# Transposing queries and keys as unsplit float32 values, two heads to a block, and splitting them from PSUM

## The chip, the cores and the metric

The kernel runs on one core of one Trainium2 chip. The metric is device time in microseconds (us). A core has five engines that work from their own instruction streams, in order, and wait for each other by semaphores: PE (matrix products and transposes, results in PSUM), DVE (vector operations), ACT (activation functions and copies), POOL and SP (here mostly DMA and some adds). PSUM is a small memory of eight banks of 128 x 512 float32 from which DVE and ACT read PE's results.

## The reference

The program is an encoder of two layers on x[512, 1024]. Each layer computes, in float32 accuracy:

```python
xn = rms_norm(x, norm1_g[l])
aq, ak, av, bq, bk, bv, cq, ck, cv, cg, gates = jnp.split(xn @ w_in[l], split_pts, axis=-1)
aq = apply_rope(rms_norm(aq, a_q_norm_g[l]), ...)      # ak, bq, bk in the same way; 64 columns a head
ya = dilated_mixer(aq, ak, av)                         # A: 6 heads, 3 waves of 2
yb = diff_attention(bq, bk, bv, lam)                   # B: 4 heads with two softmax maps each, 4 waves
cq, ck = apply_rope(cq), apply_rope(ck) * 64 ** -0.5   # C: retention, 4 heads, 2 waves of 2
yc = silu(cg) * rms_norm(bidirectional_retention(cq, ck, cv, ...))
g = sigmoid(gates)
x = x + (g0 * (ya @ w_br_a[l]) + g1 * (yb @ w_br_b[l]) + g2 * (yc @ w_br_c[l])) @ w_o[l]
x = x + square(relu(rms_norm(x, norm2_g[l]) @ w_mlp1[l])) @ w_mlp2[l]
```

Scores are products of queries and keys over the 64 columns of a head, so queries and keys must come to PE with those columns on the partitions. They are computed with tokens on the partitions and have to be transposed.

## The kernel before

**Split numbers.** PE takes reduced float32 (fp32r) at full rate. Every large product is therefore done on two parts of each factor, a high part (the value rounded to fp32r) and a low part (the rest): high x high, high x low and low x high, added up in PSUM. Weights arrive by DMA as `raw`; ACT writes `whi` and DVE `wlo` (`refine`, L261), one unit ahead of their use.

**The main stream.** `gemm` (L273) does a chunk of a product: four PSUM banks (`acc`, a pool of four, L125), four units of weights, and a yield after each bank of each unit. In the last unit a bank is evacuated as soon as it is complete. Since a chunk takes all four banks of the pool, the first matmul of the next chunk waits until the first bank of this one has been read. The order of chunks is `sequence` (L810): waves A0, A1, A2, then `cg`, C0, C1, B0, B1, gates and branch products (G, W), B2, B3, G20 and so on. A wave holds queries, keys and values of two heads (of a head with two maps for B).

**The side threads.** The work on a wave runs in four generators per layer: `thread_prep` (L790: statistics, rope and transposes of queries and keys), `thread_a`, `thread_b` (L603) and `thread_c` (L780). They are woven into the main stream when the program is written, not while it runs. `build` (L1024) keeps for each engine a sum of estimated costs (`self.cost`: a DVE operation 0.09 + columns/800, one of ACT 0.19 + columns/1000, an fp32r transpose 0.06, an fp32 one 0.11, in us) and gives out side steps, the threads in turn, as long as DVE and ACT stand more than 3 us behind PE in those sums (`SLACK`). A step that yields `("wait", name)` may go on only when PE's sum has grown by `W[name]` (4.0 for "prep", 8.0 for "yb", 6.0 for "sc").

**The exception to it.** Before wave i the main stream yields `("need", ("done", l, wave i-4))` (`LAG`, L33 and L864). While that is not met, `build` writes side steps with no regard to the sums, first those that may go on, and, where none may, by `step_side(True)`, which also disregards the waits. For B3 the need is that both heads of C1 are done; for B2 it is C0.

**Heads.** A head of C (`c_head`, L753) takes four rounds of scores, decay and products, and then `head_norm` (L568): ACT copies the result out of PSUM (`y`), PE transposes it (`ps_yt`), ACT squares and sums four blocks, DVE makes a reciprocal root in a chain of operations on 128 x 4, then `yn<-ps_yt`; after the wait "yb" PE transposes back (`ps_yb`) and DVE multiplies by the gate. `b_tail` of a head of B ends in the same way.

**The step that is changed.** `prep` (L466) is called 36 times (2 layers, 9 waves, two halves of 256 tokens). DVE applies norm and rope into `o`, [128 tokens, 2 token tiles x 2 (queries, keys) x 2 heads x 64]. ACT and DVE split it into `sp`, laid out so that a head's high and low parts stand side by side in blocks of 128 columns; eight fp32r transposes (L511) fill two PSUM banks, one for queries and one for keys. They are copied into `qk`, which has six planes of [128, 512]: for head m plane m (queries), 2+m (keys) and 4+m (keys with high and low parts exchanged). `score` (L520) multiplies whole planes m and 4+m for the two cross terms and a half of planes m and 2+m for high x high.

Of the kernel before, what the change touches and what calls it, by code (L numbers as in the profile page):

```python
# [9 lines left out]
FT = mybir.dt.float32  # L10
FR = mybir.dt.float32r
AF = mybir.ActivationFunctionType
OP = mybir.AluOpType
# [3 lines left out]
P = 128  # L17
# [46 lines left out]


def weight_plan(sequence):
    """The weight blocks in the order of use: (array, layer, first row tile, row tiles, columns per row tile)."""
    units, chunks = [], {}
    r = lambda a, n: list(range(a, a + n))
    for l in range(DEPTH):  # L70
        for s in sequence:
            kind, k0, k1, name = s[0], 0, KD, "w_in"
            if kind == "A":
                cols = [(x * 384 + s[1] * 128, 128) for x in range(3)]
            elif kind == "B":
                cols = [(1152 + x * 512 + s[1] * 128, 128) for x in range(3)]
            elif kind == "C":
                cols = [(2688 + s[1] * 128, 128), (2944 + s[1] * 128, 128), (3200 + s[1] * 256, 256)]
            elif kind == "cg":
                cols = [(3712, 512)]  # L80
            elif kind == "G":
                cols = [(4224 + s[1] * 1024 + s[2] * 512, 512)]
            elif kind == "W":
                name, cols, k1 = "w_br_" + "abc"[s[1]], [(s[2] * 512, 512)], (3, 4, 4)[s[1]]
            elif kind == "O":
                name, cols = "w_o", [(s[1] * 512, 512)]
            elif kind == "M1":
                name, cols = "w_mlp1", [(s[1] * 512, 512)]
            else:
                name, cols, k0, k1 = "w_mlp2", [(s[2] * 512, 512)], s[1] * 8, s[1] * 8 + 8  # L90
            first = len(units)
            for k in range(k0, k1, 2):
                units.append((name, l, (k, cols), min(2, k1 - k), sum(c for _, c in cols)))
            chunks[l, s] = (first, len(units))
    return units, chunks


def pack_weights(inputs, sequence):
    """Every weight block laid out as it lands on chip: row in the tile, row tile, column."""
    out = []  # L100
    for (name, l, (k, cols), n, c) in weight_plan(sequence)[0]:
        w = inputs[name][l, k * P:(k + n) * P]
# [5 lines left out]
class Trunk:  # L108
    def __init__(self, ctx, tc, a):
# [8 lines left out]
        self.up = mk("u", N_U)  # L118
        self.wp = mk("w", 1)
        self.qp = mk("qk", 2)  # L120
        self.sp = mk("sp", 2)
        self.tp = mk("tiny", 4)
        self.Tp = mk("dec", 1)
        self.dp = mk("scratch", 1, space=bass.MemoryType.DRAM)
# [114 lines left out]
            self.stt(lo, x, scale, hi.bitcast(FT), OP.mult, OP.subtract)  # L239
        return hi, lo  # L240

    # ---------------------------------------------------------------- weights
    def plan(self):
        units, self.ch = weight_plan(self.sequence)
        self.units, off = [], 0
# [52 lines left out]
                yield  # L298
            k += n

    # ---------------------------------------------------------------- set-up
    def setup(self):
        nc, a = self.nc, self.a
        cp = self.cp
# [73 lines left out]
                self.stt(S[:, :, 0:8], bc(g[:, 8:16]), -1.0, self.sinp, OP.mult, OP.mult)  # L378
                self.tt(S[:, :, 8:16], bc(g[:, 0:8]), self.sinp, OP.mult)

    # ---------------------------------------------------------------- norm of x
    def norm_open(self, which, l):
        self.nrm = {"col": which * 16 + l * 8, "xg": [None] * KD, "sq": None}

# [35 lines left out]
        self.act(rB, b2)  # L420
        return rB

    # ---------------------------------------------------------------- prep of q, k, v
    def wave_buffers(self, kind):
        w = {"kind": kind}
        w["qk"] = self.qp.tile([P, 6, SEQ], FR, tag="qk", name=self.uid("qk"))
# [39 lines left out]
    def prep(self, w, jp):  # L466
# [5 lines left out]
        if w["kind"] in "AB":  # L472
# [11 lines left out]
            o = u  # L484
            self.tt(u8, u8, rs[:, :, None].to_broadcast([P, 8, 64]), OP.mult)
        else:
# [6 lines left out]
            self.tt(oj[:, :, :, 0:32], tj[:, :, :, 32:64], bc(self.sinc[:, :, 0:32], 32), OP.mult)  # L493
            self.tt(oj[:, :, :, 32:64], tj[:, :, :, 0:32], bc(self.sinc[:, :, 32:64], 32), OP.mult)
            self.tt(o, o, u, OP.add)
        yield
        s = self.sp.tile([P, 8, 128], FR, tag="sp", name=self.uid("sp"))
        o8 = o.rearrange("p (a m d) -> p a m d", m=2, d=64)

        def hi_of(v):  # L500
            return bass.AP(tensor=v.tensor, offset=v.offset, ap=[list(v.ap[0]), [256, 4], [192, 2], [1, 64]])
        lo = s.rearrange("p (a m) d -> p a (m d)", m=2)[:, :, 64:192].rearrange("p a (m d) -> p a m d", d=64)
        self.act(hi_of(s), o8)
        self.tt(lo, o8, hi_of(s.bitcast(FT)), OP.subtract)
        yield ("wait", "prep")
        qs = slice(jp * 256, (jp + 1) * 256)
        for c in range(2):
            b = self.ps((P, 2, 256), FR, name="ps_prep")
            for m in range(2):
                for j in range(2):  # L510
                    self.tr(b[:, m, j * P:(j + 1) * P], s[:, 4 * j + 2 * c + m, :], self.identr)  # L511
            bf = b.bitcast(FT)
            self.copy(w["qk"][:, 2 * c:2 * c + 2, qs], bf, "ACT")
            if c:
                self.copy(w["qk"][0:64, 4:6, qs], bf[64:128], "DVE")
                self.copy(w["qk"][64:128, 4:6, qs], bf[0:64], "ACT")
            yield

    # ---------------------------------------------------------------- attention pieces
    def score(self, w, ms, j, pss, n=None):  # L520
        qk = w["qk"]
        js = slice(j * P, (j + 1) * P)
# [283 lines left out]
            self.flags.add(("prep", l, s[0], s[1]))  # L806
            yield

    # ---------------------------------------------------------------- main stream
    sequence = ([("A", 0), ("A", 1), ("A", 2), ("cg",), ("C", 0), ("C", 1), ("B", 0), ("B", 1),  # L810
# [188 lines left out]
        self.xt = None  # L999
        self.flags.add(("xtok",))  # L1000

    # ---------------------------------------------------------------- weaving
    def step_side(self, force=False):
        n = len(self.side)
        for i in range(n):
# [50 lines left out]


def arrange(inputs):
    """The inputs as the program takes them: the same numbers, laid out anew."""
    g = {k: np.asarray(v) for k, v in inputs.items()}  # L1060
    return {
        "x": np.ascontiguousarray(g["x"]),
# [22 lines left out]
```

## Time and profile before

| | |
|---|---|
| three runs | 1811.63 us median (1811.30 to 1813.87) |
| span of the profiled execution | 1812.9 us |
| PE busy | 1784.7 us, 98% |
| DVE busy | 1051.4 us, 58% |
| ACT busy | 795.4 us, 44% |
| POOL busy | 186.4 us, 10% |

The profile gives for its execution the span alone, from the first to the last instruction on the chip; it is 1.3 us longer than the median of the runs and within what they show. Busy times of PE include overlaps of pipelined matmuls. In a timeline row the columns are start, duration, engine, line, operation and the names out<-in; a run of equal instructions is one row with its count, and a bracket tells how long the engine sat idle before it and who released it.

### The profile page before, as it was taken

What the parts mean: (1) busy time and instruction counts of PE and PEld (TensorE: products, weight loads), DVE (VectorE), ACT (ScalarE), POOL (GpSimd) and SP (SyncE); (2) the same over time, 40 slices, a digit from 0 to 9 for tenths busy, and PEclk for the clock granted to TensorE, in tenths of its full rate; (3) what the DMA queues carried; (4) which work ended last, traced back from release to release, by engine and by line L of the source; (5) the groups of instructions that cost most, each with busy time, mean ns of one, the idle gap of its engine ahead of it and who ended that gap; (6) DMA issues with size and microseconds to landing.
All of it is one profiled execution on the core that took longest, in us unless ns stands there. A gap on an engine that the chain in (4) does not pass through costs nothing.

```text
span 1812.9 us, 22187 instructions
## 1 busy us (share of the span) xinstructions
PE 1784.7 (98%) x8433; PEld 1481.1 (82%) x8433; DVE 1051.4 (58%) x1963; ACT 795.4 (44%) x1469; POOL 186.4 (10%) x177
## 2 busy tenths in 40 slices
PE   7999999999999999999999999999999999999999
PEld 6878978877888888888888888788778878888887
DVE  7676787877465333333576767777865552233433
ACT  5555655645334332322345556455543343333241
POOL 1000000011043111111220000000111321111010
PEclk8999999999999999999999999999999999999999
DMA  6221222222233223223332112222212422323222
GB/s 223 88 70 44 85 70 62 79 70 70 82 119 125 93 93 105 93 93 104 105 105 82 65 44 85 71 64 82 80 63 91 141 80 96 102 93 97 101 94 82
DMA packets 49243, 162.78 MB, mean 90 GB/s; under 512 B 5580, under 2 KB 7792, under 8 KB 49008
## 3 DMA queue, kind: packets, MB, share of 16 engines
q1 hardware_dynamic: 45952, 151.91, 25.7%
q0 software_dynamic: 2560, 8.39, 1.4%
q8 instruction: 66, 1.08, 0.3%
q10 hardware_dynamic: 624, 1.07, 0.2%
q14 instruction: 41, 0.34, 0.1%
HBM read 155.05 MB, written 6.29 MB: 89 GB/s over the span
## 4 chain that ended last, share of the span: by engine, by line
PE 93%; DVE 4%; issue 1%; ACT 1%; POOL 0%; DMA 0%; SPq 0%; ACTq 0%; POOLq 0%; DVEq 0%
PE acc L218 81%; PE ps_c_head L218 2%; PE ps_b_scores L218 1%; PE ps_prep L222 1%; PE ps_a_tail L218 1%; PE ps_to_keys L222 1%; PE ps_b_tail L218 1%; PE ps_a_diag_scores L218 1%; PE ps_a_dense_scores L218 1%; DVE wlo L166 1%; DVE xgl L177 1%; DVE part L166 0%; DVE xr L166 0%; PE ps_yt L222 0%; PE ps_yb L222 0%
## 5 line engine op out<-in xcount | busy, mean ns | idle before, releaser
L166 DVE TENSOR_TENSOR wlo<-raw,whi 128x1024 fp32r<-128x1024 f32 (+2 forms) x296 | 351.4, 1187 | 485.9 <-ACT whi L155 484.1
L155 ACT ACTIVATE whi<-raw 128x1024 fp32r<-128x1024 f32 (+2 forms) x296 | 300.0, 1014 | 632.2 <-PE acc L218 558.2
L218 PE MATMUL acc<-xgh,whi 128*128 128x512 f32 x960 | 380.5, 396 | 0.0
L218 PE MATMUL acc<-xgl,whi 128*128 128x512 f32 x960 | 375.7, 391 | 0.0
L218 PE MATMUL acc<-xgh,wlo 128*128 128x512 f32 x960 | 374.8, 390 | 0.0
L218 PEld LDWEIGHTS acc<-xgh,whi 128*128 128x128 f32 x960 | 180.6, 188 | 39.5 <-issue 3.1
L218 PEld LDWEIGHTS acc<-xgh,wlo 128*128 128x128 f32 x960 | 180.6, 188 | 38.3
L218 PE MATMUL acc<-whi,xgh 128*128 128x384 f32 (+1 forms) x576 | 208.7, 363 | 1.5 <-DVE vl L177 0.8
L218 PEld LDWEIGHTS acc<-xgl,whi 128*128 128x128 f32 x960 | 180.8, 188 | 35.4
L218 PE MATMUL acc<-wlo,xgh 128*128 128x384 f32 (+1 forms) x576 | 202.8, 352 | 2.0 <-DVE wlo L166 2.0
L218 PE MATMUL acc<-whi,xgl 128*128 128x384 f32 (+1 forms) x576 | 201.0, 352 | 0.1
L163 POOL TENSOR_TENSOR gate<-gate,gate 128x512 f32<-128x512 f32 x32 | 50.4, 1590 | 926.5 <-DVE gate L177 562.8
L163 POOL TENSOR_TENSOR rl<-rl 128x512 f32<-128x512 f32 x64 | 78.5, 1236 | 537.4 <-ACT hh L155 429.7
L218 PEld LDWEIGHTS acc<-whi,xgh 128*128 128x128 f32 x576 | 109.6, 191 | 13.2 <-issue 5.4
L218 PEld LDWEIGHTS acc<-wlo,xgh 128*128 128x128 f32 x576 | 109.9, 191 | 7.6 <-DVE wlo L166 2.3
L218 PEld LDWEIGHTS acc<-whi,xgl 128*128 128x128 f32 x576 | 109.5, 190 | 6.5 <-issue 0.7
L218 PE MATMUL acc<-hh,wlo 128*128 128x512 f32 x256 | 99.7, 389 | 0.9 <-DVE wlo L166 0.9
L218 PE MATMUL acc<-hl,whi 128*128 128x512 f32 x256 | 99.6, 389 | 0.0
L218 PE MATMUL acc<-hh,whi 128*128 128x512 f32 x256 | 99.6, 389 | 0.0
L218 PE MATMUL acc<-whi,hh 128*128 128x512 f32 x256 | 99.6, 389 | 0.0
L218 PE MATMUL acc<-wlo,hh 128*128 128x512 f32 x256 | 99.6, 389 | 0.0
L218 PE MATMUL acc<-whi,hl 128*128 128x512 f32 x256 | 99.6, 389 | 0.0
(218 smaller groups left out, 2741.8 us busy)
## 6 DMA issues: line engine op xcount, KB each, us to landing
raw<-in_weights_dram SPq DMA_DIRECT2D x236, 512.0 KB, 3.3
raw<-in_weights_dram SPq DMA_DIRECT2D x56, 384.0 KB, 3.1
xr<-xspill POOLq DMA_DIRECT2D x16, 256.0 KB, 4.1
x<-in_x_dram SPq DMA_DIRECT2D x8, 256.0 KB, 5.8
xspill<-xt POOLq DMA_DIRECT2D x8, 256.0 KB, 3.5
xspill<-xr POOLq DMA_DIRECT2D x8, 256.0 KB, 2.3
blob<-in_blob_dram SPq DMA_DIRECT2D x1, 1024.0 KB
raw<-in_weights_dram SPq DMA_DIRECT2D x4, 256.0 KB, 2.6
```

Source lines behind the costliest of these rows:

```text
L155: self.nc.scalar.activation(out, in_, func, **k)
L163: self.nc.gpsimd.tensor_tensor(out, a, b, op=op)
L166: self.nc.vector.tensor_tensor(out, a, b, op=op)
L177: self.nc.vector.scalar_tensor_tensor(out, a, s, b, op0=op0, op1=op1)
L218: self.nc.tensor.matmul(out, lhsT, rhs, start=start, stop=stop)
L222: self.nc.tensor.transpose(out, in_, ident)
```

## The change

`prep` no longer splits before the transposes. The four blocks of 128 columns of `o` (two heads each, of one token tile's queries or keys) are transposed as float32 into one PSUM bank. Then ACT writes the high parts of each head from the bank into `qk` (two instructions on 64 partitions), DVE writes the low parts as bank minus high part into the other 64 partitions (two instructions), and for each head ACT copies the keys' high part, and DVE the keys' low part, into plane 4+m. The first yield of `prep` is gone; the wait "prep" now follows the rope directly, and there is a yield between the transposes, the high parts and the low parts. The pool `sp` is dropped. The other lines of the diff are comments and docstrings.

```diff
--- before.py
+++ after.py
@@ -118,7 +118,6 @@
         self.up = mk("u", N_U)
         self.wp = mk("w", 1)
         self.qp = mk("qk", 2)
-        self.sp = mk("sp", 2)
         self.tp = mk("tiny", 4)
         self.Tp = mk("dec", 1)
         self.dp = mk("scratch", 1, space=bass.MemoryType.DRAM)
...
@@ -493,30 +492,26 @@
             self.tt(oj[:, :, :, 0:32], tj[:, :, :, 32:64], bc(self.sinc[:, :, 0:32], 32), OP.mult)
             self.tt(oj[:, :, :, 32:64], tj[:, :, :, 0:32], bc(self.sinc[:, :, 32:64], 32), OP.mult)
             self.tt(o, o, u, OP.add)
-        yield
-        s = self.sp.tile([P, 8, 128], FR, tag="sp", name=self.uid("sp"))
-        o8 = o.rearrange("p (a m d) -> p a m d", m=2, d=64)
-
-        def hi_of(v):
-            return bass.AP(tensor=v.tensor, offset=v.offset, ap=[list(v.ap[0]), [256, 4], [192, 2], [1, 64]])
-        lo = s.rearrange("p (a m) d -> p a (m d)", m=2)[:, :, 64:192].rearrange("p a (m d) -> p a m d", d=64)
-        self.act(hi_of(s), o8)
-        self.tt(lo, o8, hi_of(s.bitcast(FT)), OP.subtract)
         yield ("wait", "prep")
         qs = slice(jp * 256, (jp + 1) * 256)
+        b = self.ps((P, 2, 256), name="ps_prep")
         for c in range(2):
-            b = self.ps((P, 2, 256), FR, name="ps_prep")
-            for m in range(2):
-                for j in range(2):
-                    self.tr(b[:, m, j * P:(j + 1) * P], s[:, 4 * j + 2 * c + m, :], self.identr)
-            bf = b.bitcast(FT)
-            self.copy(w["qk"][:, 2 * c:2 * c + 2, qs], bf, "ACT")
-            if c:
-                self.copy(w["qk"][0:64, 4:6, qs], bf[64:128], "DVE")
-                self.copy(w["qk"][64:128, 4:6, qs], bf[0:64], "ACT")
-            yield
-
-    # ---------------------------------------------------------------- attention pieces
+            for j in range(2):
+                self.tr(b[:, c, j * P:(j + 1) * P], o[:, (2 * j + c) * P:(2 * j + c + 1) * P], self.ident)
+        yield
+        qk = w["qk"]
+        own = [slice(64 * m, 64 * m + 64) for m in range(2)]
+        for m in range(2):
+            self.act(qk[own[m], m:4:2, qs], b[own[m]])
+        yield
+        for m in range(2):
+            self.tt(qk[own[1 - m], m:4:2, qs], b[own[m]], qk.bitcast(FT)[own[m], m:4:2, qs], OP.subtract)
+        for m in range(2):
+            self.act(qk[own[1 - m], 4 + m, qs], b[own[m], 1])
+            self.copy(qk[own[m], 4 + m, qs], qk.bitcast(FT)[own[1 - m], 2 + m, qs], "DVE")
+        yield
+
+
     def score(self, w, ms, j, pss, n=None):
         qk = w["qk"]
         js = slice(j * P, (j + 1) * P)
```

The costs of the steps and the yields enter the weaving, so the order of PE, DVE and ACT differs nearly everywhere behind the first `prep`; POOL's and SP's orders are unchanged. Three places are shown. Line numbers after the change are smaller by one.

**One prep on ACT**, in the first layer. Before, from the split of a rope result (`sp`) to the copies of the banks into `qk`:

```order
L155 ACTIVATE sp_738<-u_731 128x4x2x64
L155 ACTIVATE whi_741<-raw_586 128x768
L155 ACTIVATE qk_282<-ps_prep_717 128x2x256
L155 ACTIVATE qk_282<-ps_prep_723 128x2x256
L155 ACTIVATE qk_282<-ps_prep_723 64x2x256
L155 ACTIVATE whi_771<-raw_623 128x768
L155 ACTIVATE qk_282<-ps_prep_783 128x2x256
L155 ACTIVATE qk_282<-ps_prep_789 128x2x256
L155 ACTIVATE qk_282<-ps_prep_789 64x2x256
```

After, the same stretch; 64x2x256 are the high parts and 64x256 the exchanged keys:

```order
L154 ACTIVATE qk_279<-ps_prep_668 64x2x256
L154 ACTIVATE vh_452<-acc_460,nr_87_381 128x64
L154 ACTIVATE vh_452<-acc_461,nr_87_381 128x64
L154 ACTIVATE qk_279<-ps_prep_668 64x2x256
L154 ACTIVATE whi_694<-raw_529 128x768
L154 ACTIVATE qk_279<-ps_prep_668 64x256 x2
L154 ACTIVATE whi_731<-raw_583 128x768
L154 ACTIVATE qk_279<-ps_prep_755 64x2x256 x2
L154 ACTIVATE whi_774<-raw_620 128x768
L154 ACTIVATE qk_279<-ps_prep_755 64x256 x2
```

The split ahead of the transposes and the copies of whole banks have gone; four smaller ACT instructions read one bank for each `prep`.

**PE around the last head of C** in the first layer (`y` and `ps_yt` belong to head 3 of wave C1). Before, from its forward transpose:

```order
L222 MATMUL ps_yt_3359<-blob,y_3357 128x128 x4
L218 MATMUL ps_b_tail_3175<-wTl_3351,vh_1876 128x512
L218 MATMUL ps_b_tail_3175<-wTh_3350,vl_1877 128x512
L218 MATMUL ps_b_scores_3413<-qk_2132 128x512
L218 MATMUL ps_b_scores_3414<-qk_2132 128x512
L218 MATMUL ps_b_scores_3413<-qk_2132 128x512
L218 MATMUL ps_b_scores_3414<-qk_2132 128x512
L218 MATMUL acc_3479<-whi_3275,xgl_144 128x384
L218 MATMUL acc_3479<-whi_3275,xgh_159 128x384
L218 MATMUL acc_3479<-wlo_3276,xgh_159 128x384
L218 MATMUL acc_3479<-whi_3275,xgl_160 128x384
```

Its `ps_yb` stands 40 rows behind `ps_yt`, in the middle of B3's matmuls. After, the end of the stretch that the need of B3 forces out, from the forward transpose of the same head to its back transpose:

```order
L221 MATMUL ps_yt_3452<-blob,y_3450 128x128 x4
L217 MATMUL ps_b_scores_3484<-qk_2957 128x512
L217 MATMUL ps_b_scores_3485<-qk_2957 128x512
L217 MATMUL ps_b_scores_3484<-qk_2957 128x512
L217 MATMUL ps_b_scores_3485<-qk_2957 128x512
L221 MATMUL ps_to_keys_3497<-blob,e_3063 128x128
L221 MATMUL ps_to_keys_3497<-blob,e_3146 128x128
L221 MATMUL ps_to_keys_3497<-blob,e_3203 128x128
L221 MATMUL ps_to_keys_3497<-blob,e_3293 128x128
L221 MATMUL ps_yb_3506<-blob,yn_3480 128x128 x4
```

The two transposes are now nine rows apart, with no `acc` matmul between them; another pair (rows 1501 and 1508) stands just ahead at seven rows. The second layer has the same two pairs at the same distances. Ahead of B3's matmuls, and so ahead of G20, the program now also has what thread C and thread B do later in the program before.

**DVE at the evacuation of B3's first bank** (`vl`). Before:

```order
L166 TENSOR_TENSOR rt_719_3432<-rs_716_3426 128x16
L166 TENSOR_TENSOR rt_719_3432<-rt_719_3432,rh_718_3430 128x16
L177 SCALAR_TENSOR_TENSOR rs_716_3426<-rt_719_3432,rs_716_3426 128x16
L166 TENSOR_TENSOR u_3451<-u_3451,rs_716_3426 128x512
L166 TENSOR_TENSOR wlo_3599<-raw_3486,whi_3598 128x1024
L166 TENSOR_TENSOR sp_3458<-u_3451,sp_3458 128x4x128
L166 TENSOR_TENSOR u_3591<-t_3338,Cg 128x512
L166 TENSOR_TENSOR u_3591<-u_3591,sm_3593 128x8x16
L177 SCALAR_TENSOR_TENSOR vl_3477<-acc_3478,nr_87_384,vh_3476 128x128
L166 TENSOR_TENSOR u_3591<-u_3591,rs_716_3426 128x512
```

After:

```order
L165 TENSOR_TENSOR yn_3480<-ps_yt_3452,hg_3464 128x512
L192 RECIPROCAL c_749_3648<-s_715_3482 128x1
L176 SCALAR_TENSOR_TENSOR c_749_3648<-s_715_3482,nlam,c_749_3648 128x1
L176 SCALAR_TENSOR_TENSOR e_3494<-e_3494,c_749_3648,e_3491 128x512
L165 TENSOR_TENSOR wTl_3503<-ps_to_keys_3497,wTh_3502 128x512
L176 SCALAR_TENSOR_TENSOR yn_3480<-ps_yb_3506,ghead,cg_1157 128x512
L180 TENSOR_REDUCE nm_750_3664<-ps_b_scores_3665 128x1
L165 TENSOR_TENSOR ynl_3513<-yn_3480,ynh_3512 128x512
L180 TENSOR_REDUCE nm_750_3664<-ps_b_scores_3666 128x1
L176 SCALAR_TENSOR_TENSOR vl_3518<-acc_3519,nr_87_381,vh_3517 128x128
L176 SCALAR_TENSOR_TENSOR vl_3518<-acc_3520,nr_87_381,vh_3517 128x128
```

Before, the evacuation stands among operations of `prep`, with none of a head's norm in the rows just ahead. After, it stands behind both `yn` of that last head (the second waits for `ps_yb`). Between the evacuations of the first bank of B2 and of B3 DVE has 66 other instructions before and 105 after in the first layer.

## Rows read from the trace of the kernel before

**Rows 1.** The page: span, and the chain that ended last.

```profile
span 1812.9 us, 22187 instructions
...
PE 93%; DVE 4%; issue 1%; ACT 1%; POOL 0%; DMA 0%; SPq 0%; ACTq 0%; POOLq 0%; DVEq 0%
```

**Rows 2.** Windows: us, busy (count) by engine, PE clock, DMA share, GB/s.

```profile
60.00:500.00 440.00, 438.04 (x2167) 359.12 (x2166) 317.22 (x707) 234.36 (x496) 12.46 (x8) 1.00 0.23 72
327.46:353.70 26.24, 26.24 (x147) 23.27 (x147) 23.69 (x69) 16.69 (x40) 0.00 (x0) 1.00 0.24 78
1219.14:1245.52 26.38, 26.25 (x147) 23.23 (x146) 21.99 (x66) 15.13 (x38) 0.00 (x0) 1.00 0.23 76
```

**Rows 3.** Timeline of PE: fp32 transposes (ps_yt) and fp32r ones (ps_prep) among acc.

```profile
297.87 0.39 PE L218 MATMUL acc<-ynh,whi 128*128 128x512 f32 x1
298.10 0.60 PE L222 MATMUL ps_yt<-blob,y 128*128 128x128 f32 x4
298.45 0.48 PE L218 MATMUL acc<-ynl,whi 128*128 128x512 f32 x1
298.77 0.40 PE L218 MATMUL acc<-ynh,wlo 128*128 128x512 f32 x1
...
300.85 0.39 PE L218 MATMUL acc<-ynh,wlo 128*128 128x512 f32 x1
301.08 0.79 PE L222 MATMUL ps_prep<-identr,sp 128*128 128x128 f32 x8
301.71 0.47 PE L218 MATMUL acc<-ynh,whi 128*128 128x512 f32 x1
302.01 0.40 PE L218 MATMUL acc<-ynl,whi 128*128 128x512 f32 x1
```

**Rows 4.** Groups of ACT and DVE by line and shape: busy us, mean ns.

```profile
L155 ACT ACTIVATE qk<-ps_prep 64x512 fp32r<-64x512 f32 x36 | 21.3, 591 | 15.6 <-DVE qk L214 15.2
L155 ACT ACTIVATE vh<-acc,nr 128x64 fp32r<-128x64 f32 x48 | 14.0, 321 | 1.3 <-DVE vl L177 1.2
L214 DVE CAST qk<-ps_prep 64x512 fp32r<-64x512 f32 x36 | 25.0, 694 | 8.2 <-ACT qk L155 6.9
L177 DVE SCALAR_TENSOR_TENSOR vl<-acc,nr,vh 128x64 fp32r<-128x64 f32 x48 | 12.3, 280 | 3.7 <-ACT vh L155 3.4
```

**Rows 5.** Critical chain of 325 to 360: last head of C and its neighbours.

```profile
335.69 0.44 PE ps_yt L222 x4
...
336.60 0.89 PE ps_b_scores L218 x4
...
343.17 0.60 PE ps_yb L222 x4
```

**Rows 6.** Timeline: a head_norm of B from ps_yt to yn, on PE and DVE.

```profile
474.56 0.60 PE L222 MATMUL ps_yt<-blob,y 128*128 128x128 f32 x4
...
478.81 0.69 DVE L166 TENSOR_TENSOR yn<-ps_yt,hg 128x512 f32<-128x512 f32 x1
```

**Rows 7.** Groups of DVE by line and shape that recur in the stretch.

```profile
L166 DVE TENSOR_TENSOR wlo<-raw,whi 128x1024 fp32r<-128x1024 f32 x236 | 294.1, 1246 | 448.0 <-ACT whi L155 446.6 <-PE acc L218 0.5
...
L166 DVE TENSOR_TENSOR wTl<-ps_to_keys,wTh 128x512 fp32r<-128x512 f32 x48 | 33.0, 687 | 14.7 <-ACT wTh L155 14.7
...
L166 DVE TENSOR_TENSOR rt<-rt,rh 128x4 f32<-128x4 f32 x60 | 9.7, 162 | 2.0
```

**Rows 8.** Timelines: B2's first bank complete, B3's first evacuation, G20's first matmul.

```profile
324.78 0.34 PE L218 MATMUL acc<-whi,xgl 128*128 128x384 f32 x1
...
353.70 0.34 DVE L177 SCALAR_TENSOR_TENSOR vl<-acc,nr,vh 128x128 fp32r<-128x128 f32 x1
...
355.45 0.39 PE L218 MATMUL acc<-xgh,whi 128*128 128x512 f32 x1
```

**Rows 9.** A wait of PE in the second layer, and the window behind it.

```profile
1459.18 1.56 PE L222 MATMUL ps_thread_xtok<-blob,xr 128*128 128x128 f32 x12 [2.56 <-DVE xtok L214]
...
1460.60:1464.00 3.40, 3.40 (x11) 2.63 (x10) 0.69 (x1) 0.31 (x1) 0.00 (x0) 0.50 0.00 0
```

## The prediction, as it was put on record before the change was run

> **What bounds the kernel now.** I read the engine totals first, then windows, then the chain that ended last, then timelines of PE and DVE where the order changes. PE is the bound: 93% of the chain is PE [rows 1], and between 60 and 500 us of the first layer, where all calls of `prep` of that layer lie, PE is busy for 438.04 of 440 us at a granted clock of 1.00, the upper of its two levels, 2.4 GHz [rows 2]. DVE is busy for 317 us there, 72%, ACT for 234. So a change saves what it takes off PE, and it costs whatever makes PE wait; DVE and ACT time as such is covered. One stretch is near another limit: from the evacuation of B2's first bank to that of B3's DVE is busy for 23.69 of 26.24 us, and in the second layer for 21.99 of 26.38 [rows 2], and PE still has no pause. There any further DVE work has 10 to 15% of room.
>
> **Term 1: transposes on PE, a gain.** Eight fp32r transposes per `prep` become four fp32 ones. Neighbouring `acc` matmuls start 0.23 us apart. From 300.85 to 302.01 there are two such steps and the eight transposes: 1.16 - 0.46 = 0.70 us. From 297.87 to 298.77 there are two steps and four fp32 transposes, those of `ps_yt`, which use the same identity and the same shapes as the new ones: 0.90 - 0.46 = 0.44 us [rows 3]. The saving is 0.26 us, times 36 calls 9.4 us. Where the eight stood in two pieces it is a little more, since a piece costs a hand-over of its own; the order has both forms, and I keep 11 us as the other end.
>
> The row shows that an fp32 transpose is 0.11 us against 0.09, a factor of 1.25. The Trainium skill (FP8 and Floating Point Precision, section TensorE Precision Notes) says that true float32 takes four passes through the PE array, which speaks against this change: by it four fp32 transposes would be as long as sixteen passes. The trace disagrees for transposes, and the sum goes by the row.
>
> **Term 2: the other edits of a `prep`, taken as zero.** ACT loses two copies of a bank and the split of `o`, and gets two high parts on 64 x 512 (0.59 each) and two copies of 64 x 256; the latter are not in the trace and lie between 0.32 (128 x 64) and 0.59 (64 x 512) [rows 4]. ACT becomes lighter by roughly half a microsecond a call, beside PE. DVE loses the low part of `o` (512 columns, 0.69 [rows 7]) and a CAST of 64 x 512 (0.69 [rows 4]), and gets two subtractions of 512 columns (0.69 each by the same rows) and two CASTs of 64 x 256, which are between 0.28 (64 columns) and 0.69 (512) [rows 4]; I take 0.35, half of the CAST of twice the columns. So DVE gains work of 0.6 to 1.4 us a call, about 25 us over 36 calls. Its cover is PE's 438 us in the window against DVE's 317; it is gone only in the stretch of term 3, where these instructions are counted. The new order within a call (high part on ACT, then low part on DVE from the same bank, then the exchanged keys on ACT) adds two waits. Queued behind them on ACT and DVE are `whi` and `wlo` of the next unit of weights, for which PE waits; they are written one unit, 24 matmuls of 0.23 us or 5.5 us, ahead. Two subtractions of 0.69 are inside that. One bank instead of two is held, for longer; I see no reason for a pause or a gain. Zero, with -2 and +4 us as ends.
>
> **Term 3: steps forced out ahead of B3, a loss, and it decides the sign.** The new costs and yields shift the weaving. When the main stream comes to B3, which needs both heads of C1, thread C is about 16 steps further behind than before, and the rule that gives out side steps regardless of the sums writes some 47 at once instead of 11, in each layer. The rows of the order show the end of it: `ps_yt` of the last head and its `ps_yb` stand 9 rows apart instead of 40, and the pair ahead of it 7 rows.
>
> What that distance is worth: before, the last head's `ps_yt` is at 335.69 and its `ps_yb` at 343.17, 7.5 us of other PE work [rows 5]. The chain between them (ACT squares, thirteen DVE operations on 128 x 4, `yn`) is 4.9 us long when nothing else is queued: 474.56 to 478.81 + 0.69 = 479.50 [rows 6]. So it is hidden before. In the new order the two pairs have only about 2 us of PE work between them each. PE executes in order, so it waits in `ps_yb`, twice per layer, and what is queued behind is the rest of heads B and C, then G20.
>
> Size, by DVE. Between the evacuations of the first banks of B2 and B3 DVE has 105 instructions instead of 66 in the first layer. The 39 more are: 19 of 512 columns (four low parts, decay and split of C, scores' maxima, `yn`, `ynl`) at 0.69, 13.1 us; one `wlo` of 1024, 1.25; four CASTs at 0.35, 1.4; 15 of one to four columns at 0.16, 2.4 [rows 7]. Together 18.1 us. Neighbours overlap a little: the instructions of the old stretch sum to 28.4 us by the means of their groups, and DVE was busy for 23.69 [rows 2], a factor of 0.83. So the stretch becomes 15.1 to 18.1 us longer; I take 17, nearer the upper end, since with waits the old stretch took 26.24 us.
>
> PE gets more work ahead of G20 too, which hides part of it: 14 score matmuls at 0.22 (0.89 for four [rows 5]) 3.1 us, six products at 0.23 1.4, 24 transposes at 0.11 (0.44 for four) 2.6, and a second `prep` 0.2: 7.3 us, and with a hand-over of 0.1 us between kinds at eleven places 8.4. G20's first matmul, at 355.45, needs the bank whose evacuation ended at 353.70 + 0.34 = 354.04: a margin of 1.4 us [rows 8]. And the new stretch starts later: the evacuation of B2's first bank stands behind the maximum of a score pair whose matmuls are 4.1 us behind the bank's last one (16 matmuls of 384 columns at 0.17, four transposes, four scores); before it is 327.46 - 325.1 = 2.4 us [rows 2, 8]. So G20 is late by 17.0 - 8.4 - 1.4 + 1.7 = 8.9 us. In the second layer the same count gives 101 instructions and an elapsed time 16 us longer, so about the same. Twice 9 is 18 us.
>
> A bound that doesn't rest on DVE's load: the two chains stand one behind the other. 4.9, `ps_yb` 0.44, three products 0.69, the copy `y` 0.6, 4.9 again, `ps_yb` 0.44, then `yn` 0.7, `ynh` 0.6, two ACT reads of the bank at 0.3 to 0.5 each and `vl` 0.35 come to 14.3 us; the PE work in that stretch is 8.3. That leaves at least 6 us per layer, 12 in all. The upper end, with `wlo` and four `prep` instructions queued inside the first chain and nothing overlapping, is 12 us per layer.
>
> **Term 4: the clock after a wait, a small loss.** After PE waited for 2.56 us at 1459.18, the granted clock was 0.50, the 1.2 GHz level, for 3.40 us, in which 11 matmuls took twice their time: 1.7 us lost [rows 9]. The waits of term 3 are about as long and come in pairs. Between 0 and 3.4 us for two layers; I take 1.8.
>
> **Sum.** Against the profiled execution: 1812.9 - 9.4 + 0 + 18.0 + 1.8 = 1823.3. Its span is 1.3 us above the median of the runs, so 1822.0 us.
>
> **Rivals.**
> 1. *The forced steps are hidden.* The mechanism that would make the kernel faster: DVE's work for the forced steps is done while PE still has B3's long matmuls, because DVE runs ahead at 72% load, and the chains are short since ACT is lighter; G20 then isn't late. It decides if PE loses under 3 us per layer. Against it stands the 90% in just this stretch [rows 2], for it only that neighbouring instructions may overlap more than the factor 0.83. Time: 1812.9 - 9.4 - 1.3 = 1802.2, faster.
> 2. *Only the chain bound.* DVE packs as tightly as 0.83 and only the two chains show: 6 to 7 us per layer and no fall of the clock, so +13: 1815.2, and with one of the two chains hidden (-3 per layer) 1809. This is no measurable change or just beyond it.
> 3. *The tail is worse.* Each chain has other DVE and ACT work in it, 12 us per layer, and the clock falls in both layers, 3.4: 1812.9 - 9.4 + 24 + 3.4 - 1.3 = 1829.6.
> 4. *Float32 transposes cost four times an fp32r one.* 4 x 4 x 0.088 = 1.4 us a call instead of 0.70, +25 us where term 1 has -9.4: 1856. Against it stand rows 3 with the same shapes. The rule named above would give this.
>
> **How the numbers follow.** The forecast (stalls of 7 to 11 us per layer) has 0.55, with its own range 1817 to 1827. Hidden 0.13, chain bound only 0.15, worse 0.16, four times 0.01. A measurement of this kernel can tell some 0.2%, 3.6 us, so no change is 1808.0 to 1815.3. Faster: rival 1, 0.13. Same: most of rival 2, 0.12. Slower: the rest, 0.75. The range 1804 to 1831 leaves out the hidden case and the far end of the worse one, under 2 in 10, and holds the ends of term 2.
>
> **What would show it.** Term 1: the bracket around `ps_prep` x4 is 0.44 us, 36 of them. Term 2: ACT is about 17 us less busy, DVE about 25 more, and no new wait of PE for `wlo` or `whi` outside the two stretches. Term 3: PE waits for DVE `yn` in `ps_yb` twice per layer shortly before the end of B3's part, and `acc` of G20 waits for `vl`, 7 to 11 us together; the other pairs of `ps_yt` and `ps_yb`, 33 to 51 rows apart, show nothing. Term 4: a PEclk of 0.50 behind it. The forecast is wrong if the window from B3's last matmul to G20's first holds under 3 us of idle PE per layer, or if PE loses more than 3 us to waits that are in none of these places.

## The result, and the profile after

The changed kernel takes 1843.25 us (median of four runs, 1841.87 to 1844.24), the kernel before 1811.47: a ratio of 1.0169, 95% interval 1.0155 to 1.0184, 31.8 us slower. The forecast was 1822.0, within 1804 to 1831: the direction holds, the size is three times the one forecast, and the result lies above the range.

The page of the changed kernel, its span and its chain; PE has 4 points less of the chain than in [rows 1], and DVE has 2 and ACT 1 of them:

```profile
span 1840.0 us, 21998 instructions
...
PE 89%; DVE 6%; ACT 2%; issue 1%; POOL 0%; DMA 0%; SPq 0%; DVEq 0%; ACTq 0%; POOLq 0%
```

PE's waits by instruction and releaser (us in total, times, longest). Before, no `ps_yb` is in this view:

```profile
PE ps_yb L221 <- DVE yn L165: 14.3, 3, 5.5
...
PE ps_yb L221 <- DVE c L192: 3.4, 1, 3.4
```

The place is the forecast one. B3's first matmul starts at 326.50 (before: 333.90) and G20's at 376.16 (355.45): that stretch has grown from 21.55 to 49.66 us, in the second layer to 49.23. Some of the growth is work that stood elsewhere before: PE is busy for 39.5 us in it now. The windows of these two stretches, with columns as in [rows 2]:

```profile
326.50:376.16 49.66, 39.49 (x181) 29.96 (x179) 40.10 (x107) 28.07 (x70) 0.00 (x0) 0.86 0.16 53
1229.96:1279.19 49.23, 39.66 (x180) 30.37 (x179) 37.60 (x104) 26.28 (x67) 0.00 (x0) 0.82 0.15 54
```

PE is idle for 10.2 and 9.6 us, and its mean clock is 0.86 and 0.82. DVE, which the forecast took to be at its limit here, is busy for 81 and 76% only. The timeline of PE shows the end of the stretch in the first layer:

```profile
351.62 0.60 PE L221 MATMUL ps_yt<-blob,y 128*128 128x128 f32 x4
...
359.83 1.08 PE L221 MATMUL ps_yb<-blob,yn 128*128 128x128 f32 x4 [5.53 <-DVE yn L165]
360.99 0.80 PE L217 MATMUL ps_c_head<-wTh,vh 128*128 128x512 f32 x1
361.72 0.79 PE L217 MATMUL ps_c_head<-wTl,vh 128*128 128x512 f32 x1
...
363.62 1.11 PE L221 MATMUL ps_yt<-blob,y 128*128 128x128 f32 x4 [0.69 <-ACT y L154]
...
370.77 0.95 PE L221 MATMUL ps_yb<-blob,yn 128*128 128x128 f32 x4 [3.41 <-DVE c L192]
...
376.16 0.50 PE L217 MATMUL acc<-xgh,whi 128*128 128x512 f32 x1 [0.45 <-DVE vl L176]
```

The reader is to see a ladder: transpose forward, wait, transpose back, twice, with G20's first matmul at its foot. From 351.62 to 376.16 are 24.5 us; the PE work in them was put at 8.3 in the forecast. The second wait is put down to `c`; the timeline of DVE has the `yn` of this pair end at 370.62, 0.15 us before `ps_yb`, and it is the real releaser:

```profile
369.93 0.69 DVE L165 TENSOR_TENSOR yn<-ps_yt,hg 128x512 f32<-128x512 f32 x1
370.54 0.15 DVE L192 RECIPROCAL c<-s 128x1 f32<-128x1 f32 x1
```

Behind the waits PE runs at half clock: for 10.2 and 3.4 us in the first layer, and in the second for 20.5 us without a break. The windows:

```profile
357.30:367.50 10.20, 6.76 (x19) 3.75 (x19) 7.16 (x14) 5.25 (x14) 0.00 (x0) 0.50 0.15 51
370.90:374.30 3.40, 3.40 (x10) 2.06 (x9) 3.03 (x6) 1.27 (x4) 0.00 (x0) 0.50 0.00 0
1261.80:1282.30 20.50, 14.98 (x41) 9.46 (x42) 13.71 (x42) 10.72 (x32) 0.00 (x0) 0.50 0.08 27
```

In the second layer PE is busy for all the 5.10 us from the last `ps_yb` to G20, so there it is the half-speed PE, and not DVE, that sets G20's start:

```profile
1274.09 1.09 PE L221 MATMUL ps_yb<-blob,yn 128*128 128x128 f32 x4 [3.27 <-DVE yn L165]
...
1279.19 0.78 PE L217 MATMUL acc<-xgh,whi 128*128 128x512 f32 x1
```

DVE in the first chain, from the first operation on 128x4 to `yn`:

```profile
353.49 0.16 DVE L176 SCALAR_TENSOR_TENSOR hf<-yss,hq 128x4 f32<-128x4 f32 x1 [1.91 <-ACT y L154]
...
354.73 0.68 DVE L165 TENSOR_TENSOR qk<-ps_prep,qk 64x512 fp32r<-64x512 f32 x1
355.44 0.16 DVE L165 TENSOR_TENSOR rt<-hg 128x4 f32<-128x4 f32 x1
355.64 0.69 DVE L165 TENSOR_TENSOR qk<-ps_prep,qk 64x512 fp32r<-64x512 f32 x1
...
357.47 1.22 DVE L165 TENSOR_TENSOR wlo<-raw,whi 128x1024 fp32r<-128x1024 f32 x1
...
358.99 0.69 DVE L165 TENSOR_TENSOR yn<-ps_yt,hg 128x512 f32<-128x512 f32 x1
```

`ps_yt` to the end of `yn` takes 8.1 us here, against 4.9 in [rows 6]: the new prep's subtractions and CASTs and a `wlo` stand between the small operations. But 4.9 us was another head's. The last head of C itself took 6.3 us in the kernel before, 335.53 to 341.80:

```profile
335.53 0.60 PE L222 MATMUL ps_yt<-blob,y 128*128 128x128 f32 x4
...
341.11 0.69 DVE L166 TENSOR_TENSOR yn<-ps_yt,hg 128x512 f32<-128x512 f32 x1
```

The transposes do what was forecast. The bracket around four of them: 88.40 - 87.50 - 0.46 = 0.44 us, where the eight took 0.70 [rows 3]:

```profile
87.50 0.39 PE L217 MATMUL acc<-xgh,whi 128*128 128x512 f32 x1
87.73 0.60 PE L221 MATMUL ps_prep<-blob,u 128*128 128x128 f32 x4
88.08 0.48 PE L217 MATMUL acc<-xgl,whi 128*128 128x512 f32 x1
88.40 0.39 PE L217 MATMUL acc<-xgh,wlo 128*128 128x512 f32 x1
```

### The profile page after: what moved, and what is told of

It is laid out like the page before. It is cut to its first block, busy times and chain, and to the rows that moved or that the text cites. A ratio compares the mean times of both kernels' runs of the same rounds, so it can differ in the third digit from the quotient of the medians.

```text
span 1840.0 us, 21998 instructions
## 1 busy us (share of the span) xinstructions
PE 1790.8 (97%) x8289; PEld 1477.1 (80%) x8289; DVE 1067.4 (58%) x2035; ACT 787.5 (43%) x1469; POOL 183.9 (10%) x177
## 4 chain that ended last, share of the span: by engine, by line
PE 89%; DVE 6%; ACT 2%; issue 1%; POOL 0%; DMA 0%; SPq 0%; DVEq 0%; ACTq 0%; POOLq 0%
PE acc L217 78%; PE ps_c_head L217 2%; PE ps_b_scores L217 2%; PE ps_b_tail L217 1%; PE ps_to_keys L221 1%; DVE wlo L165 1%; PE ps_a_tail L217 1%; PE ps_a_diag_scores L217 1%; PE ps_prep L221 1%; DVE qk L165 1%; PE ps_a_dense_scores L217 1%; DVE xgl L176 1%; DVE rt L165 0%; ACT whi L154 0%; DVE part L165 0%
## 5 line engine op out<-in xcount | busy, mean ns | idle before, releaser
L165 DVE TENSOR_TENSOR wlo<-raw,whi 128x1024 fp32r<-128x1024 f32 (+2 forms) x296 | 355.2, 1200 | 498.4 <-ACT whi L154 496.0
```

The lines of the kernel that those rows point to most:

```text
L165: self.nc.vector.tensor_tensor(out, a, b, op=op)
```

## The experiments

The change is two things at once: another prep, and another weaving that follows from its yields and charges. The first two runs take them apart.

**New prep, old weaving.** A yield in front again, transposes and high parts in one step, and each step charged what the old step was:

```diff
+        yield
+        self.cost["ACT"] += 0.702
+        self.cost["DVE"] += 0.73
         yield ("wait", "prep")
+        kept = dict(self.cost)
...
+        self.cost.update(kept)
+        self.cost["PE"] += 0.24
+        self.cost["ACT"] += 0.702
         yield
```

> The changed prep, with the yields of the old one and with its steps charged to the sums at the old costs, so that the weaving comes out as before (the need of B3 forces 12 steps again, the last head's back transpose stands as far behind as before). Theory (the loss is the forced steps alone, the transposes gain 9.4 us): 1811.5 - 9.4 = 1802 us, between 1799 and 1806. Rival (the new prep itself makes PE wait, by its longer chain through one bank or its 25 us more of DVE): above 1811 us, with waits of PE for wlo, whi or qk outside B3.

Measured: 1811.19 us, ratio 0.9994 (0.9985 to 1.0003), no change. The loss is gone, but so is the gain of 9.4. PE has new waits of about 1 us, the largest, once in each layer, in front of a `ps_yb`. This run, then the same head in the kernel before:

```profile
294.92 0.61 PE L221 MATMUL ps_yt<-blob,y 128*128 128x128 f32 x4
...
302.19 0.69 DVE L165 TENSOR_TENSOR yn<-ps_yt,hg 128x512 f32<-128x512 f32 x1
...
303.03 0.63 PE L221 MATMUL ps_yb<-blob,yn 128*128 128x128 f32 x4 [1.21 <-DVE yn L165]
```

```profile
305.28 0.68 DVE L166 TENSOR_TENSOR yn<-ps_yt,hg 128x512 f32<-128x512 f32 x1
...
307.02 0.60 PE L222 MATMUL ps_yb<-blob,yn 128*128 128x128 f32 x4
```

From `ps_yt` to the end of `yn` are 8.0 us here and 7.9 before (from 298.10 [rows 3]): this chain is not longer. PE has less to do beside it, eleven `acc` matmuls and four transposes fewer, so the order is not quite the old one in this place. The rival is right in part, since the new prep loses its own gain; where it loses it, this run doesn't show.

**Old prep, new weaving.** Split ahead of the wait, the two banks in the two steps behind it, charged as the changed steps are:

```diff
-        yield
...
+        self.cost.update(kept)
         yield ("wait", "prep")
...
+        self.cost["PE"] += 0.44
         yield
...
+        self.cost["ACT"] += 1.404
         yield
+        self.cost["ACT"] += 0.892
+        self.cost["DVE"] += 2.28
+        yield
```

> The old prep (split first, eight fp32r transposes, two banks) with the yields and charged costs of the changed one, so that the weaving forces 44 steps ahead of B3 as in the changed kernel. Theory (forced steps alone): the changed kernel's loss without the transposes' gain, 1843 + 9.4 = 1852 us, between 1846 and 1858. Rival (the new prep's DVE instructions in the stretch make the loss): 1815 to 1830 us.

Measured: 1846.40 us, ratio 1.0188 (1.0174 to 1.0203), 34.8 us slower than before. So the weaving alone makes the whole loss, without any instruction of the new prep: 17.4 us a layer. The new prep in this weaving gains 1846.4 - 1843.25 = 3.2 us. That difference is small beside the noise: the intervals of the two kernels overlap. PE waits in the same `ps_yb`: DVE `yn` 8.8 us in three, `c` 3.4 in one. The first wait of a layer is 2.75 us, where the changed kernel has 5.5:

```profile
355.27 0.66 PE L222 MATMUL ps_yt<-blob,y 128*128 128x128 f32 x4 [0.49 <-ACT y L155]
...
361.00 1.09 PE L222 MATMUL ps_yb<-blob,yn 128*128 128x128 f32 x4 [2.75 <-DVE yn L166]
```

**Other charges at the end of `prep`, so that less is forced in the first layer.**

```diff
+        self.cost["DVE"] -= 0.82
+        self.cost["ACT"] += 0.5
```

> The changed kernel, with 0.82 us less DVE and 0.5 us more ACT charged to the sums per prep. The weaving then forces 10 steps ahead of B3 in the first layer (back transposes 50 rows behind) and 22 in the second (8 and 8 rows). Theory: the first layer ends 4.7 us earlier than that of the unchanged kernel, the second has a loss of at most 18 us: about 1811.5 - 9.4 + 18 = 1820 us, 1812 to 1822. Rival (the loss isn't tied to the forced steps): 1835 to 1845 us.

Measured: 1818.12 us, ratio 1.0023 (1.0011 to 1.0036), as in the theory, but not as it said. In the emitted order of the second layer the back transposes have other PE work ahead of them, so hardly a chain is exposed there; the first layer, expected to gain, ends 6.9 us later than before, through waits of 0.5 to 2 us spread over it. The sum of the theory came out by two errors.

**Side steps given out earlier.**

```diff
-SLACK = -3.0
+SLACK = 1.0
```

> The changed kernel with SLACK 1.0 instead of -3.0, so that side steps are given out while DVE and ACT stand up to 1 us ahead of PE in the sums; 2 and 10 steps are forced ahead of B3 in the two layers, no back transpose is nearer than 40 rows. Theory: 1802 us as with the old weaving, 1799 to 1808. Rival (side work given out earlier makes PE wait elsewhere): 1808 to 1820 us.

Measured: 1829.74 us, ratio 1.0098 (1.0084 to 1.0112). Nothing much is forced at B3, and it is 18 us slower: the rival, beyond its range. Getting rid of the forced steps isn't enough; PE's waits are now spread over `ps_yb`, `acc` for `vl` and `ps_to_keys`.

**The need of B3 steps thread C alone.** `build` first advances the thread whose head is missing:

```diff
-                if not self.step_side() and not self.step_side(True):
+                if not self.step_for(need) and not self.step_side() and not self.step_side(True):
```

> The changed kernel, in which an unmet need of B3 steps thread C alone, so that ahead of B3 5 us of PE work and 9 of DVE are forced (21 and 29 before) and one pair of transposes stands without other PE work between, none at 8 or 9 rows. Theory (the loss is DVE's queue and two exposed chains): one exposed chain of 5 us per layer, a fall of the clock of 1.7, and 3.5 of small waits elsewhere, less 4.7: 1811.5 + 11 = 1822 us, 1816 to 1828. Rival (the exposed chain alone costs as much as the whole, since the queue is hidden): 1835 us or more.

Measured: 1824.49 us, ratio 1.0073 (1.0056 to 1.0091). Steps forced and loss fall together. The sum was right and its parts were not: PE waits for only 0.4 us in `ps_yb`, and the largest wait is now that of a prep's transposes for their rope result, which was left behind:

```profile
PE ps_prep L221 <- DVE u L165: 6.0, 2, 3.0
```

**DVE's load under the old prep.** The kernel before, with two idle copies at the end of each prep:

```diff
+                pad = self.tiny(512, "pad", 2)
+                for m in range(2):
+                    self.nc.vector.tensor_copy(pad[64 * m:64 * m + 64, 256 * m:256 * m + 256], w["qk"].bitcast(FT)[64 * m:64 * m + 64, 2 + m, qs])
```

> The kernel before, with two more DVE CASTs of 64x256 (0.3 us each, to a buffer that nobody reads) at the end of each prep, the sums not charged, so the weaving is unchanged; DVE's load per prep is then that of the changed one. Theory (the changed prep's gain is eaten by DVE work behind the transposes, which delays the chains of head_norm and others): 1814 to 1818 us. Rival (DVE has room, 72%; the loss lies in the longer chain ACT, DVE, ACT through one bank): 1811 to 1812.5 us.

Measured: 1818.05 us, ratio 1.0033 (1.0021 to 1.0045), 6.7 us slower. 72 copies of 0.29 us on an engine that is 72% busy cost a third of their 20.5 us. Where PE pays for them is not shown: among its waits is no `ps_yb`, and none that is new is longer than 0.6 us.

**The low copies on POOL**, new prep, old weaving:

```diff
-            self.copy(qk[own[m], 4 + m, qs], qk.bitcast(FT)[own[1 - m], 2 + m, qs], "DVE")
+            self.nc.gpsimd.tensor_copy(qk[own[m], 4 + m, qs], qk.bitcast(FT)[own[1 - m], 2 + m, qs])
```

> The changed prep in the old weaving (1811.2 us), with the two copies of the keys' exchanged low part on POOL instead of DVE, which is then as loaded per prep as in the kernel before. Theory (DVE's load behind the transposes eats the gain): 1804 to 1808 us, under both kernels. Rival (chain through the bank, or POOL's copies too slow for the scores): 1810 us or more.

Measured: 1806.78 us, ratio 0.9970 (0.9959 to 0.9982): faster than both kernels, 4.5 us under the kernel before. A copy is twice as long on POOL, and no wait of PE for it is in the view. In the groups by line and shape (as [rows 4]), of this run and of the changed kernel:

```profile
L518 POOL CAST qk<-qk 64x256 fp32r<-64x256 f32 x72 | 42.5, 590 | 652.7 <-DVE qk L165 652.4
```

```profile
L213 DVE CAST qk<-qk 64x256 fp32r<-64x256 f32 x72 | 20.6, 286 | 1.1
```

**The low copies on ACT**, else the same (`"DVE"` becomes `"ACT"`).

> As the run with the two copies of the keys' low part on POOL (1806.8 us; changed prep, old weaving), but with these copies on ACT, which has 16 us less work than in the kernel before. Theory (DVE's load behind the transposes is what matters, any other engine will do): 1805 to 1808 us. Rival (ACT's own queue, with whi and the exponentials, makes PE wait): 1809 us or more.

Measured: 1810.37 us (1806.92 to 1812.71), ratio 0.9987 (0.9979 to 0.9996). That is 1.2 us under the kernel before, in the rival's range, and not to be told from the copies on DVE (1811.19). Why ACT serves less well than POOL was not followed up.

**The low copies on POOL in the weaving that their charges give.**

```diff
+            self.cost["POOL"] += 0.59
+            self.nc.gpsimd.tensor_copy(qk[own[m], 4 + m, qs], qk.bitcast(FT)[own[1 - m], 2 + m, qs])
```

> The changed kernel with the two copies of the keys' low part on POOL and nothing else: yields and cost formulas as in the changed kernel, POOL's copies charged to POOL. DVE's sum per prep is then that of the kernel before; the weaving forces 10 and 18 steps ahead of B3, and no pair of transposes stands near another. Theory: the loss of the forced steps is gone, 1805 to 1812 us. Rival (the weaving is worse in other places too, as in the run with one layer's forced steps, 1818): 1814 to 1820.

Measured: 1823.47 us, ratio 1.0051 (1.0036 to 1.0066), above both ranges. My statement that no pair stands near another was wrong: in the second layer one forward and one back transpose are apart by eleven matmuls and a prep, away from B3, and PE waits there:

```profile
1096.74 0.60 PE L221 MATMUL ps_yt<-blob,y 128*128 128x128 f32 x4
...
1099.10 0.60 PE L221 MATMUL ps_prep<-blob,o 128*128 128x128 f32 x4
1104.03 0.45 PE L221 MATMUL ps_yb<-blob,yn 128*128 128x128 f32 x1 [4.33 <-DVE yn L165]
```

So the same copies give 1806.8 or 1823.5, by the weaving alone.

**The low copies on POOL in the weaving of the changed kernel** (charged to DVE as before, by `self._d`).

> The changed kernel with the two copies of the keys' low part on POOL, still charged to DVE, so that the weaving (44 forced steps, pairs at 8 to 10 rows) stays that of the changed kernel. Theory (the loss by DVE's load per prep and the loss of the forced steps add up): as between the two kernels in the old weaving, 4.4 us less than the changed kernel, 1837 to 1840.5 us. Rival (in the forced stretch the chains are all, and DVE's load elsewhere has no part): 1842 us or more. Second rival (DVE's queue in the forced chains is a large part of the loss): 1834 us or less.

Measured: 1837.30 us, ratio 1.0135 (1.0118 to 1.0152), 6.0 us under the changed kernel. Of these 1.9 are in `ps_yb`, where PE waits for 15.8 us instead of 17.7. The two copies per prep are worth 4 to 7 us of DVE's load in either weaving; they add to the forced steps.

**The transposes twice**, new prep, old weaving:

```diff
-                self.tr(b[:, c, j * P:(j + 1) * P], o[:, (2 * j + c) * P:(2 * j + c + 1) * P], self.ident)
...
+                for _ in range(2):
+                    self.tr(b[:, c, j * P:(j + 1) * P], o[:, (2 * j + c) * P:(2 * j + c + 1) * P], self.ident)
```

> The changed prep in the old weaving (1811.2 us), with each of its four transposes issued twice into the same place. Prices a transpose in its surroundings: at 0.11 us, 36 x 4 x 0.11 = 15.8 us more, 1825 to 1829. Rival (PE has slack in these places and the price of transposes isn't felt, which would explain why the change in the old weaving gained little): 1812 to 1818.

Measured: 1825.08 us, ratio 1.0069 (1.0056 to 1.0083), 13.9 us over the single ones: 144 transposes at 0.097 us. PE's time in these places is felt in full, and the price is near that of the rows (0.11).

**Idle matmuls in the forced waits.** In the changed kernel, ahead of the two forced back transposes of a layer (30 and 20 of them; the bank is overwritten by the transposes):

```diff
+        if self.forcing:
+            hi = next(iter(self.hl.values()))[0]
+            self.fills = getattr(self, "fills", 0) + 1
+            for _ in range(FILL[1 - self.fills % 2]):
+                self.nc.tensor.matmul(b2[:, 0:384], hi[:, 0, 0:P], hi[:, 0, 0:384], start=True, stop=True)
```

> The changed kernel, with idle matmuls (128x384, results overwritten at once) on PE ahead of the two forced back transposes of each layer: 30 and 20 of them, about 5.2 and 3.5 us, as long as PE's two waits there (5.5 and 3.4 us). Theory (part of the loss is the granted clock, which falls after these waits; 3 to 4 us per layer are lost at 0.50): PE stays at clock 1.00 and the kernel gains 5 to 8 us on 1843, to 1835 to 1838. Rival (waits alone): the fillers change nothing or cost 1 to 3 us, 1843 to 1846.

Measured: 1847.52 us, ratio 1.0196 (1.0182 to 1.0210), 4.3 us slower still. The experiment is inconclusive: the second group needs a PSUM bank that came free only when the wait was over, so it ran behind the wait. The next one keeps the first group alone. But the run shows the links behind the first `ps_yb` with PE at full clock (1.00 in each):

```profile
360.54 0.60 PE L222 MATMUL ps_yb<-blob,yn 128*128 128x128 f32 x4
...
362.52 0.66 PE L222 MATMUL ps_yt<-blob,y 128*128 128x128 f32 x4
...
374.54 0.60 PE L222 MATMUL ps_yb<-blob,yn 128*128 128x128 f32 x4
...
378.58 0.50 PE L218 MATMUL acc<-xgh,whi 128*128 128x512 f32 x1 [1.26 <-DVE vl L177]
```

```profile
368.56 0.69 DVE L166 TENSOR_TENSOR yn<-ps_yt,hg 128x512 f32<-128x512 f32 x1
```

From `ps_yb` to the next `ps_yt` are 2.0 us, from there to the end of `yn` 6.7, and from the last `ps_yb` to G20 4.0; in the changed kernel they are 3.8, 7.0 and 5.4. That is 3.4 us less, although a `wlo` of 1.2 us is queued in each of the last two.

> The changed kernel with 30 idle matmuls (128x384, 5.2 us) ahead of the first forced back transpose of each layer only. Theory (clock): PE comes out of the first wait at 1.00 instead of 0.50, some 2 us per layer, 1838 to 1841 us. Rival: no gain, 1843 or more.

Measured: 1843.61 us, ratio 1.0172 (1.0159 to 1.0185), the time of the changed kernel. PE does come out of the first wait at full clock. A window, PE, and the first `yn` on DVE:

```profile
360.00:364.00 4.00, 3.63 (x23) 3.15 (x23) 2.95 (x5) 3.53 (x5) 0.00 (x0) 1.00 0.00 0
```

```profile
355.55 5.48 PE L593 MATMUL ps_yb<-whi 128*128 128x384 f32 x30
360.87 0.60 PE L222 MATMUL ps_yb<-blob,yn 128*128 128x128 f32 x4
...
369.88 1.09 PE L222 MATMUL ps_yb<-blob,yn 128*128 128x128 f32 x4 [4.12 <-DVE c L193]
```

```profile
356.34 0.69 DVE L166 TENSOR_TENSOR yn<-ps_yt,hg 128x512 f32<-128x512 f32 x1
```

This doesn't price the clock. The first `yn` is ready at 357.03, and the fillers hold its `ps_yb` until 360.87, for 3.8 us, and as long in the second layer. So what the clock may have given back, the fillers may have taken. The order is another as well: six `acc` matmuls of B3 stand behind the first `ps_yb` now, and the `wlo` that was queued in the first chain stands ahead of its DVE operations. The second wait is 4.12 us instead of 3.41, and behind it the clock is 0.50 up to G20 and beyond.

## Why the prediction was wrong

In medians of runs the forecast was +10.4 us and the result +31.8. The two runs that take weaving and prep apart divide the miss of 21.3 us: the weaving alone costs 34.8 where terms 3 and 4 had 19.8, which is 15.0; the prep, in the new weaving, gains 3.2 where terms 1 and 2 had 9.4, which is 6.2. Each part is uncertain by some 3 us, as the intervals show.

**Term 1, the transposes: right.** The bracket is 0.44 us, and doubling them costs 0.097 us for each. The four passes of the Trainium skill (FP8 and Floating Point Precision, TensorE Precision Notes) are not what transposes show here: 0.097 us against 0.09 for fp32r.

**Term 2, the other edits at zero: wrong, by 6 us.** The step that failed is "Its cover is PE's 438 us in the window against DVE's 317". A share of 72% hides work only if it can be placed freely. In the new weaving the place is seen. With the old prep, which has one DVE instruction of 0.69 us behind its transposes, the first forced `ps_yb` comes 5.7 us behind its `ps_yt`, and PE waits for 2.75. With the new prep, which has four, 1.95 us (means of 0.689 and 0.286), and with a `wlo` of 1.2 that has come between, it comes 8.2 us behind and PE waits for 5.5. In two layers that is 5.6 us, nearly all of the 6.2. In the old weaving the price is measured but not the place: the load added to the old prep costs 6.7 us, and taken off the new one it gives back 4.4 (6.0 in the new weaving). The CAST itself is 0.29 us, at the low bound; by the page DVE is busy for 1067.4 us, 16.0 more than before, and ACT for 787.5, 7.9 less. After POOL has taken the copies, 4.5 of the 9.4 us arrive; what takes the other 4.9 was not tried out (the subtractions still stand behind the transposes).

**Term 3, the forced steps: the place and the mechanism were right, the size was not.** PE waits where it was said, in two `ps_yb` per layer, and in the first layer in G20's `acc`. The step that failed is "Size, by DVE": it made the stretch between the two evacuations 17 us longer, as if DVE's load set its length. It is 23.5 us longer in the first layer (326.04 to 375.76, 49.72 us instead of 26.24), and DVE is busy for only 40.2 of the 49.72. What sets it is the chain itself, and the bound of 14.3 us, which was there for it, took each link at its undisturbed length. The trace of the kernel before spoke against that: among its sixteen heads 4.9 us is the shortest chain from `ps_yt` to `yn` and 7.9 the longest. In the changed kernel the same links come to 24.5 us. The first is 8.2 instead of 4.9, by 1.95 of prep and 1.2 of `wlo` queued in it. From there to the next `ps_yt` are 3.8 instead of 1.7, with PE at half clock. The second chain is 7.1 instead of 4.9, by scores' maxima that are queued in it and wait for the half-speed PE. From the last `ps_yb` to G20 are 5.4 instead of 2.9, for the same reasons. Less the 8.3 us of PE work that the forecast put there, this is 16.2 us a layer instead of 6. With the old prep in the new weaving the links come to 22.3 us, which leaves 14.0 of the 17.4 measured; where the rest lies was not followed up. How much each queued instruction adds was not tested one by one.

**Term 4, the clock: much too small, and not a term beside the chain.** It had 3.4 us at 0.50 after a wait, and 1.8 us lost in all. The windows show 13.6 and 20.5 us at 0.50 in the two layers, and PE is busy for 25.1 of them. The pages of the new prep in the old weaving and of the changed kernel have the same PE instructions:

```profile
PE 1775.4 (98%) x8289; PEld 1469.2 (81%) x8289; DVE 1072.9 (59%) x2035; ACT 785.0 (43%) x1469; POOL 186.4 (10%) x177
```

```profile
PE 1790.8 (97%) x8289; PEld 1477.1 (80%) x8289; DVE 1067.4 (58%) x2035; ACT 787.5 (43%) x1469; POOL 183.9 (10%) x177
```

Their spans are 1808.8 and 1840.0 us. So of 31.2 us between them 15.4 are longer busy time of the same instructions, and 15.8 idle time. Not all of the 15.4 would come back at full clock, since the links through DVE and ACT stay. An estimate is the 3.4 us of the run with both groups of fillers, some 7 us for two layers; its order is not quite the same. No run isolates the price of the clock, so how the 15.0 us of the weaving divide between queued work and half-speed PE stays open.

**The rivals.** The hidden case and the chain bound alone are excluded, and doubling the transposes excludes the factor of four; the worse tail came nearest, and even it ended at 1829.6. A range that stopped near there was too narrow for a stretch in which the orders of three engines were new.

## What to carry to other kernels

When an edit changes the charges or yields from which a planner weaves the program, test the new order and the new instructions apart, by charging the new steps at the old prices: here the order cost 35 us and the instructions gained 3. Size an exposed chain by its links with everything that the new order queues between them, and with PE at the clock that a wait leaves it, not by the load of its engines. A filler that is to hold the clock tells what the clock is worth only if it is over when the wait is. And before putting work on an engine that is 72% busy, look at what stands beside it in its queue: the same copies, twice as long on the idle POOL, turned no gain into 4.5 us in the old weaving.

## What the runs showed of the hardware beyond that

An fp32 transpose of 128x128 costs 0.097 us in place (0.11 in the bracket of four) against 0.09 for one in fp32r, so that a block of two heads in fp32 beats two split ones. Behind waits of 5.5 and 3.3 us in the second layer the granted clock stayed at 0.50, the 1.2 GHz level, for 20.5 us, and PE was busy for 15.0 of them. Idle matmuls of 5.3 us in place of the first wait kept it at 1.00 behind that wait; it fell in the next. A POOL copy of 64x256 with a change of partitions took 0.59 us, on DVE 0.29, on ACT (from PSUM) 0.38.
